# Strassen's scheme for part of the blocks of an MLP down projection, with the row scale on the activations

## The chip, the cores and the metric

The kernel runs on one core of a Trainium2 chip. The metric is device time in microseconds (us) of one execution, the median of several runs. Engines are named as in the profile: PE is TensorE's matmul stream and PEld its weight loads, DVE is VectorE, ACT is ScalarE, POOL is GpSimd, SP is SyncE, whose queue issues the loads of weights.

## The reference

Two layers over 256 tokens of width 2048: a convolution module, an MLP, latent attention, an MLP, and a last norm. Everything is float32. What the change touches is the MLP:

```python
def rms_norm(x, g):
    y = x * lax.rsqrt(jnp.mean(x * x, axis=-1, keepdims=True) + NORM_EPS)
    return y * g

def sq_relu_mlp(h, w1, w2):                      # w1: 2048 x 8192, w2: 8192 x 2048
    return jnp.square(jax.nn.relu(h @ w1)) @ w2

for layer in range(2):
    ...                                          # the token mixer
    h = rms_norm(x, norm_mlp_g[layer])
    x = x + sq_relu_mlp(h, mlp_w1[layer], mlp_w2[layer])
return rms_norm(x, final_norm_g)
```

The scale of the norm is a factor r per token, and squared ReLU lets it pass as r * r: it can be applied after the down projection, or to the squared activations.

## The kernel before

**Numbers in two parts.** Matmuls take operands in a reduced float32 form (F32R). Each operand is split in an upper part `hi` and a rest `lo = x - hi`, and a product of two operands is three matmuls (hi hi, lo hi, hi lo), added up in PSUM: `mm3`, lines 196 to 198. The split of weights is one copy on ACT (line 163) and one subtraction on DVE (line 167) for each half of a loaded piece. Pieces are 1 MB: four k-tiles of 128 rows by 512 columns. There are three buffers for raw pieces and `WB = 6` each for the upper and lower halves of a piece, so a half can be split when the half six places before it has been used.

**The MLP, `mlp` (line 453).** It works in two halves of 4096 hidden columns. In each half the up projection makes 8 groups of four blocks (128 hidden columns each); a group takes four loaded pieces and 64 pairs of matmuls (lines 476 and 477) into four banks of PSUM, with the weights as the stationary operand, so that the result is turned: hidden columns on the partitions, 256 tokens along the row. Then, for two blocks at a time, ACT and DVE add the two terms into `v` (488, 489), DVE squares after the ReLU (490), and the result is split into `gh` and `gl` (492, 493), which stay in SBUF for all groups of the half.

The down projection is `product_A` (line 398). For each of the four column blocks `n` of 512 it opens two accumulators, one per 128 tokens (`t`), and runs over the half's 32 k-tiles, in units of one loaded piece: 4 k-tiles x 2 token tiles x 3 matmuls = 24 matmuls of 128x128 by 128x512. Here the activations are the stationary operand. After a column block, `add` (line 373) adds the accumulator into the residual `xs`, multiplied by the row scale `r2`, which is worked out at the end of the first half's up projection (line 497). In the second half `prepare` also takes each finished column block on: its squares for the next norm on ACT (line 394) and, in layer 0, the block turned for the next layer (`turn_block`: 16 DVE transposes of 32x256 at line 317, then an upper part on ACT and a lower part on DVE for each of four k-tiles, lines 202 and 209). These are put into a list, `steps`, and `step(n)` sends off the next few between the units. In layer 1 the last column block is ordered by tokens and cut in halves, so that `finish` can begin early.

**Order.** The convolution and the attention have an order written out by hand. In the MLP the framework's scheduler sets each engine's order: among the instructions that it expects to be ready it takes the one that stands first in the program. Each engine then works in that order. PSUM has eight banks: six for accumulators and two for transposes from the convolution's end on (`repool`, line 964).

Of the kernel before, what the change touches and what calls it, by code (L numbers as in the profile page):

```python
# [10 lines left out]
F32 = mybir.dt.float32  # L11
F32R = mybir.dt.float32r
# [6 lines left out]
P = 128  # L19
# [21 lines left out]
PAD_O = 56  # L41
WB = 6
LOOK = WB // 2 - 1


SIDE = {KC - 3: 2, KC - 2: 4}
# [29 lines left out]
def trunk_kernel(  # L76
# [35 lines left out]
    def repool(name, **banks):  # L112

        psum_cx[0].close()
        psum_cx[0] = ExitStack()
        for kind, n in banks.items():
            psum[kind] = psum_cx[0].enter_context(tc.tile_pool(name=kind + name, bufs=n, space=PSUM, reuse_waits="tile"))

# [22 lines left out]
        return psum["acc"].tile([P, NB], F32, tag="acc", name=nm("acc"))  # L141

    def tr_tile():
        return psum["tr"].tile([P, NB], F32, tag="tr", name=nm("tr"))

    def load(srcs, nj, parts=1):
# [248 lines left out]

        return ssq, add, prepare

    def product_A(w, k_lo, nk, hi, lo, add, prepare, blocks=range(NNB), due=(), finish=None, before=None):


        due = list(due)
        for n in blocks:
            ps = [acc_tile() for _ in range(T)]

            n_end = 3 if finish is not None and n == blocks[-1] else 0
            wjs = []

            def products(u, t, to_end=True):
                for j in range(4):
                    k = 4 * u + j  # L410
                    mm3(ps[t], hi(k, t), lo(k, t), *wjs[u](j), k == 0, k == nk - 1 - 4 * (not to_end))

            for u in range(nk // 4):
                wjs.append(load_split([rows(w, k_lo + 4 * u, 4, n * NB, NB)], 4))
                if u < nk // 4 - n_end:
                    for j in range(4):
                        k = 4 * u + j
                        for t in range(T):
                            mm3(ps[t], hi(k, t), lo(k, t), *wjs[u](j), k == 0, k == nk - 1)
                while due:  # L420
                    prepare(due.pop(0))
                step(-(-20 * 4 // nk) + 1 if nk > 4 * NNB else 6)
                if u == 0 and n_end:
                    before()
            if n_end:
                for t in range(T):


                    halves = t == T - 1
                    for u in range(nk // 4 - n_end, nk // 4 - halves):  # L430
                        products(u, t, not halves)
                    add(n, ps, t)
                    if not halves:
                        prepare(n, t)
                    else:
                        h = NB // 2
                        for c in range(2):
                            o = acc_tile()[:, :h]
                            for j in range(4):
                                k = nk - 4 + j  # L440
                                wh, wl = (w[:, c * h : (c + 1) * h] for w in wjs[-1](j))
                                mm3(o, hi(k, t), lo(k, t), wh, wl, j == 0, j == 3)
                            add(n, {t: o}, t, c)
                            prepare(n, t, c)
                    finish(t)
            else:
                for t in range(T):
                    add(n, ps, t)
                due.append(n)
        while due:  # L450
            prepare(due.pop(0))

    def mlp(layer, ssq, next_gain, finish=None, before=None, beside=None):

        with ExitStack() as cx:
            mp = cx.enter_context(tc.tile_pool(name=f"mp{layer}", bufs=1, reuse_waits="tile"))
            nkh = FF // P // HALVES
            r2 = small.tile([P, T], F32, tag="r2", name=nm("r2"))
            nssq = None
            turned = None if next_gain is None else mp.tile([P, NB // P, S], F32, name=nm("turned"))  # L460
            for hf in range(HALVES):
                hh, hl = [], []
                for g in range(nkh // 4):
                    ps = [acc_tile() for _ in range(4)]
                    c0 = (hf * nkh + 4 * g) * P
                    for u in range(KC // 4):
                        if u == KC // 4 - 1:
                            step()
                        wj = load_split([rows(mlp_w1[layer], 4 * u, 4, c0, NB)], 4)
                        for j in range(4):  # L470
                            k = 4 * u + j
                            wh, wl = wj(j)
                            for b in range(4):
                                bs = slice(b * P, (b + 1) * P)

                                nc.tensor.matmul(ps[b], wh[:, bs], xhl(k), start=k == 0, stop=False)  # L476
# [5 lines left out]
                    gh = mp.tile([P, 4, S], F32R, tag="gh", name=nm("gh"), bufs=nkh // 4)  # L482
                    gl = mp.tile([P, 4, S], F32R, tag="gl", name=nm("gl"), bufs=nkh // 4)
                    for b2 in range(2):
                        v = mp.tile([P, 2, S], F32, tag="v", name=nm("v"), bufs=2)
                        for b in range(2):
                            o = ps[2 * b2 + b]
                            nc.scalar.activation(v[:, b, :], o[:, S:], AF.Copy)  # L488
                            nc.vector.tensor_tensor(v[:, b, :], o[:, :S], v[:, b, :], op=ALU.add)
                        nc.vector.scalar_tensor_tensor(out=v, in0=v, scalar=0.0, in1=v, op0=ALU.max, op1=ALU.mult)  # L490
                        bs = slice(2 * b2, 2 * b2 + 2)
                        nc.scalar.activation(gh[:, bs, :], v, AF.Copy)
                        nc.vector.tensor_tensor(gl[:, bs, :], v, gh[:, bs, :].bitcast(F32), op=ALU.subtract)
                    hh.append(gh)
                    hl.append(gl)
                if hf == 0:
                    r = rms_rstd(ssq[:, :, :NNB], NNB, D, "n")
                    nc.vector.tensor_tensor(r2, r, r, op=ALU.mult)
                nssq, add, prepare = residual_stage(
                    hf == HALVES - 1, next_gain, r2, turned, () if turned is None else range(NNB - 1)  # L500
                )
                product_A(
                    mlp_w2[layer],
                    hf * nkh,
                    nkh,
                    lambda k, t: hh[k // 4][:, k % 4, t * P : (t + 1) * P],
                    lambda k, t: hl[k // 4][:, k % 4, t * P : (t + 1) * P],
                    add,
                    prepare,
                    finish=(lambda t: finish(nssq, t)) if finish is not None and hf == HALVES - 1 else None,  # L510
                    before=lambda: before(nssq),
                )
            return nssq


# [1151 lines left out]
```

## Time and profile before

| | |
|---|---|
| time, median of 3 runs (lowest to highest) | 1975.28 us (1975.23 to 1975.32) |
| span of the profiled execution, first to last instruction (it has no time of its own beside it) | 1973.7 us |
| mean granted TensorE clock | 0.999 |
| DMA traffic | 367.58 MB, mean 186 GB/s |
| layer 0's MLP in the span (up, down, up, down) | from 300.3 to 1003.5 us |
| layer 1's MLP in the span | from 1262.3 to 1965.9 us |

The span is divided by engine into busy shares; a busy PE counts overlapping matmuls once. "x" is a count, and in a group's row the numbers are busy time and the mean duration in ns of one instruction, then the idle time of the engine just before the group's instructions and what ended it. In the rows of windows, each engine has its busy time and number of instructions, followed by the granted clock, the share of DMA time and GB/s. A row of a timeline has start, length, engine, line, operation, and what was written from what.

### The profile page before, as it was taken

The page shows a single profiled execution, that of the slowest core. Times are in us where ns is not written, and L with a number is a line of the kernel's source. Part 1 is how long each engine was busy: PE and PEld are TensorE (multiplying, and loading weights), DVE is VectorE, ACT ScalarE, POOL GpSimd, SP SyncE. Part 2 cuts the span into 40 slices and gives each one's busy share as a digit, 9 for nine tenths or more (in the row PEclk, how much of TensorE's full clock was granted, in tenths as well). Part 3 has the DMA queues.
Part 4 walks back from the last instruction along what each step waited for, and adds up shares of the span by engine and source line. Part 5 has one row for each costly group of instructions (what it writes and reads, how often), then busy time and mean ns, then how long its engine had stood idle before and what let it go on. Part 6 is the DMA issues. An engine that isn't in the chain of part 4 may idle for free.

```text
span 1973.7 us, 27791 instructions
## 1 busy us (share of the span) xinstructions
PE 1958.3 (99%) x10963; PEld 1716.5 (87%) x10963; DVE 1267.0 (64%) x1920; ACT 987.3 (50%) x1426; POOL 220.7 (11%) x172
## 2 busy tenths in 40 slices
PE   8999999999999999999999999999999999999998
PEld 8999888888888888888899998888888888888887
DVE  7999987755444556666656666866555445665554
ACT  5667755544333445444456655554443334544442
POOL 6999100000000000000002310000000000000000
PEclk9999999999999999999999999999999999999999
DMA  7765556565556666556554445666555566665553
GB/s 231 208 189 175 181 181 205 187 189 191 194 196 194 188 189 188 192 190 197 187 182 140 138 150 173 209 195 192 192 192 192 192 192 192 192 192 192 192 192 107
DMA packets 243875, 367.58 MB, mean 186 GB/s; under 512 B 15512, under 2 KB 90528, under 8 KB 243488
## 3 DMA queue, kind: packets, MB, share of 16 engines
q1 hardware_dynamic: 242416, 363.28, 57.7%
q10 hardware_dynamic: 1328, 2.52, 0.4%
q8 instruction: 86, 1.41, 0.3%
q14 instruction: 45, 0.37, 0.0%
HBM read 363.68 MB, written 2.10 MB: 185 GB/s over the span
## 4 chain that ended last, share of the span: by engine, by line
PE 95%; DVE 2%; ACT 1%; DMA 0%; issue 0%; POOL 0%; ACTq 0%; DVEq 0%
PE acc L476 23%; PE acc L196 15%; PE acc L198 15%; PE acc L197 15%; PE acc L477 12%; PE acc L581 8%; PE acc L1044 2%; DVE sum L668 1%; DMA xs<-in_x 0%; PE acc L1427 0%; PE tr L260 0%; ACT hi L163 0%; PE acc L1291 0%; PE acc L1293 0%; PE acc L1292 0%
## 5 line engine op out<-in xcount | busy, mean ns | idle before, releaser
L167 DVE TENSOR_TENSOR lo<-raw,hi 128x1024 fp32r<-128x1024 f32 (+1 forms) x631 | 760.8, 1211 | 637.4 <-ACT hi L163 632.3
L163 ACT ACTIVATE hi<-raw 128x1024 fp32r<-128x1024 f32 (+1 forms) x696 | 722.2, 1045 | 759.5 <-PE acc L197 428.1
L476 PE MATMUL acc<-xt,hi 128*128 128x512 f32 x2048 | 710.2, 390 | 0.0
L477 PE MATMUL acc<-xt,lo 128*128 128x256 f32 x2048 | 577.5, 282 | 0.0
L476 PEld LDWEIGHTS acc<-xt,hi 128*128 128x128 f32 x2048 | 384.4, 188 | 80.6
L197 PE MATMUL acc<-hi,gl 128*128 128x512 f32 (+1 forms) x1028 | 399.1, 388 | 0.0
L198 PE MATMUL acc<-lo,gh 128*128 128x512 f32 (+1 forms) x1028 | 399.1, 388 | 0.0
L196 PE MATMUL acc<-hi,gh 128*128 128x512 f32 (+1 forms) x1028 | 399.1, 388 | 0.0
L477 PEld LDWEIGHTS acc<-xt,lo 128*128 128x128 f32 x2048 | 387.1, 189 | 0.2
L198 PEld LDWEIGHTS acc<-lo,gh 128*128 128x128 f32 x1028 | 193.0, 188 | 40.1
L196 PEld LDWEIGHTS acc<-hi,gh 128*128 128x128 f32 x1028 | 193.0, 188 | 39.8
L197 PEld LDWEIGHTS acc<-hi,gl 128*128 128x128 f32 x1028 | 193.0, 188 | 39.3
L581 PE MATMUL acc<-xt,hi 128*128 128x256 f32 x1024 | 180.1, 281 | 0.3 <-ACT b L863 0.2
L668 DVE SCALAR_TENSOR_TENSOR sum<-ub,w_dw,sum 128x256 f32<-128x256 f32 x409 | 164.3, 483 | 3.5 <-ACT sum L638 3.0
L167 POOL TENSOR_TENSOR lo<-raw,hi 128x1024 fp32r<-128x1024 f32 x65 | 155.0, 2410 | 17.5 <-ACT hi L163 17.5
L581 PEld LDWEIGHTS acc<-xt,hi 128*128 128x128 f32 x1024 | 154.6, 188 | 1.1 <-ACT xt L847 0.6
L581 PE MATMUL acc<-xt,lo 128*128 128x256 f32 x512 | 139.2, 279 | 0.0
L581 PEld LDWEIGHTS acc<-xt,lo 128*128 128x128 f32 x512 | 94.6, 188 | 0.0
L1222 POOL MEMSET pad_kv<- 128x8 f32 x1 | 0.1, 106 | 770.5 <-DVE xt L209 770.5
L488 ACT ACTIVATE v<-acc 128x256 f32<-128x256 f32 x128 | 46.3, 381 | 25.4 <-PE acc L477 25.4
L196 PE MATMUL acc<-hi,oh 128*128 128x512 f32 x128 | 50.6, 395 | 0.0
L198 PE MATMUL acc<-lo,oh 128*128 128x512 f32 x128 | 50.0, 390 | 0.0
(279 smaller groups left out, 1719.9 us busy)
## 6 DMA issues: line engine op xcount, KB each, us to landing
raw<-in_mlp_w SPq DMA_DIRECT2D x256, 1024.0 KB, 5.1
raw<-in_conv_w_pw SPq DMA_DIRECT2D x62, 512.0 KB, 5.0
raw<-in_conv_w_pw SPq DMA_DIRECT2D x16, 1024.0 KB, 5.0
raw<-in_mla_w_o SPq DMA_DIRECT2D x16, 1024.0 KB, 5.5
raw<-in_mla_w_kv_up SPq DMA_DIRECT2D x8, 1024.0 KB, 5.7
raw<-in_mla_w_in SPq DMA_DIRECT2D x8, 576.0 KB, 3.7
raw<-in_mla_w_in SPq DMA_DIRECT2D x4, 1024.0 KB
raw<-in_mla_w_q_up SPq DMA_DIRECT2D x16, 256.0 KB, 3.2
```

The lines of the kernel that those rows point to most:

```text
L163: nc.scalar.activation(hi, raw[:, js, :], AF.Copy)
L167: eng.tensor_tensor(lo, raw, hi.bitcast(F32), op=ALU.subtract)
L196: nc.tensor.matmul(ps, sh, mh, start=start, stop=False)
L197: nc.tensor.matmul(ps, sl, mh, start=False, stop=False)
L198: nc.tensor.matmul(ps, sh, ml, start=False, stop=stop)
L476: nc.tensor.matmul(ps[b], wh[:, bs], xhl(k), start=k == 0, stop=False)
L477: nc.tensor.matmul(ps[b][:, :S], wl[:, bs], xh(k), start=False, stop=k == KC - 1)
L488: nc.scalar.activation(v[:, b, :], o[:, S:], AF.Copy)
L581: nc.tensor.matmul(pss[c][b][:, :S], w[i][:, bs], (xh, xl)[j](k), start=k == i + j == 0, stop=end and k == k0 + nk - 1 and (i, j) == terms ...
L668: nc.vector.scalar_tensor_tensor(out=out, in0=ubs[c][:, w : w + S], scalar=tap(c, w), in1=base, op0=ALU.mult, op1=ALU.add)
L1044: nc.tensor.matmul(ps2[b][t], x_kt(k, t), w[:, bs], start=k == g == i == 0, stop=k == KC - 1 and i == len(group) - 1,)
L1222: nc.gpsimd.memset(pad_kv, 0.0)
```

## The change

Strassen's scheme (in Winograd's variant) multiplies a 2 x 2 by a 2 x 2 matrix of blocks with 7 block products in place of 8. Here the left matrix is two token tiles by two k-tiles of activations, and the right one is two k-tiles by two column blocks of 512 of the weights.

- `MIXED` names, for each layer and half, the groups (of four k-tiles) that are multiplied in this way: three of eight, and two of eight in layer 0's second half. A group has two quads (two k-tiles each). The other groups are plain.
- In the up projection, the squared activations are multiplied by the row scale (`r2_row`, spread over the partitions by two transposes on PE and a copy), ahead of their split. The scale is worked out after the first group instead of at the end of the half, and `add` no longer has it. For mixed groups `mixed_inputs` makes seven combinations of 128x128 per quad, four of them by sums on DVE, and splits them.
- The down projection takes column blocks in pairs, in units of two k-tiles by 1024 columns (again 1 MB). `Sums` opens eight accumulators, four for the outputs (`e`) and four that are shared between outputs (`u`). Mixed and plain units alternate while there are mixed ones. A mixed unit makes the seven combinations of weights (`mixed_weights`: four copies on ACT, four subtractions and three combinations on DVE) and 21 matmuls. `join` adds the four shared sums into the outputs, after the last mixed unit and before the last plain ones: one copy on ACT, eight additions on DVE.
- In each layer's second half, column blocks 2 and 3 go through `product_A` as before, one after the other, with the mixed units for both in between the units of column block 2.
- PSUM in the MLP is one pool of eight accumulator banks, and transposes take theirs from it; a new pool of six and two is opened for the attention.

The diff, cut to its core:

```diff
+MIXED = {(0, 0): (0, 2, 4), (0, 1): (0, 2), (1, 0): (0, 2, 4), (1, 1): (0, 2, 4)}
+N_MIXED = 3
...
     def tr_tile():
+        if "tr" not in psum:
+            return acc_tile()
...
+    def turns_on(due, prepare, n=4):
+
+        if due and not steps:
+            prepare(due.pop(0))
+        step(n)
+
+    def mixed_weights(raw):
...
+        def halves(src):
+            hi = wpool.tile(list(src.shape), F32R, tag="hi", name=nm("hi"), bufs=WB)
+            lo = wpool.tile(list(src.shape), F32R, tag="lo", name=nm("lo"), bufs=WB)
+            nc.scalar.activation(hi, src, AF.Copy)
+            nc.vector.tensor_tensor(lo, src, hi.bitcast(F32), op=ALU.subtract)
+            return [(hi[:, i, :], lo[:, i, :]) for i in range(src.shape[1])]
+
+        b11, b21 = halves(raw[:, :, :NB])
+        (b22,) = halves(raw[:, 1:2, NB:])
+        top = raw[:, 0, :].rearrange("p (c n) -> p c n", c=2)
+        low = raw[:, 1, :].rearrange("p (c n) -> p c n", c=2)
+        nc.vector.tensor_tensor(top, raw[:, :, NB:], top, op=ALU.subtract)
+        nc.vector.tensor_tensor(low[:, 1, :], low[:, 1, :], top[:, 0, :], op=ALU.subtract)
+        nc.vector.tensor_tensor(low[:, 0, :], low[:, 0, :], low[:, 1, :], op=ALU.subtract)
+        t1, t3 = halves(top)
+        t4, t2 = halves(low)
+        return b11, b21, b22, t1, t2, t3, t4
+
+    def mixed_inputs(v, fh, fl):
...
+        halves(a[:, 0:1, :], 0, 1)
+        halves(a[:, 2:4, :], 1, 2)
+        nc.vector.tensor_tensor(a22, a21, a22, op=ALU.add)
+        nc.vector.tensor_tensor(a21, a11, a21, op=ALU.subtract)
+        nc.vector.tensor_tensor(a11, a22, a11, op=ALU.subtract)
+        nc.vector.tensor_tensor(a12, a12, a11, op=ALU.subtract)
+        halves(a, 3, 4)
+
+    class Sums:
...
+            self.u = [acc_tile() for _ in range(4)]
+            self.e = [[acc_tile() for _ in range(2)] for _ in range(T)]
...
+        def mixed(self, w, k, fh, fl, end):
+
+            b11, b21, b22, t1, t2, t3, t4 = mixed_weights(load([rows(w, k, 2, self.n * NB, 2 * NB)], 2))
+            u1, u6, u7, u5 = self.u
+            work = [
+                (u1, 0, b11), (u5, 6, t1), (u7, 4, t3), (u6, 3, t2),
+                (self.e[0][0], 1, b21), (self.e[0][1], 5, b22), (self.e[1][0], 2, t4),
+            ]
+            if self.begun:
+                work = [work[i] for i in (0, 4, 5, 1, 2, 6, 3)]
+            for ps, i, (wh, wl) in work:
+                mm3(ps, fh[:, i, :], fl[:, i, :], wh, wl, self.first(ps), end and any(ps is u for u in self.u))
+
+        def plain(self, w, k, hi, lo, k0, end):
+
+            at_j = split(load([rows(w, k, 2, self.n * NB, 2 * NB)], 2), nc.vector)
+            order = [(j, c, t) for j in range(2) for c in range(2) for t in range(T)]
+            if end:
+                order.sort(key=lambda r: r[1:])
...
+        def join(self, pool):
...
+            nc.scalar.activation(a, u1, AF.Copy)
+            tt(x(0, 0), u1, x(0, 0), op=ALU.add)
+            tt(a, u6, a, op=ALU.add)
+            tt(b, u7, a, op=ALU.add)
+            tt(a, u5, a, op=ALU.add)
+            tt(x(1, 0), b, x(1, 0), op=ALU.add)
+            tt(b, u5, b, op=ALU.add)
+            tt(x(0, 1), a, x(0, 1), op=ALU.add)
+            tt(x(1, 1), b, x(1, 1), op=ALU.add)
...
+            repool(f"mlp{layer}", acc=8)
...
+                    if hf == g == 0:
+                        scales()
...
+                        nc.vector.tensor_tensor(v, v, row, op=ALU.mult)
+                        if g in mixed:
+                            mixed_inputs(v, gh[:, b2], gl[:, b2])
+                            continue
...
+                for n in range(0, NNB - 2 * last, 2):
+                    sums = Sums(n)
+                    ks = [4 * g + 2 * b for g in plain for b in range(2)]
+                    for i, k in enumerate(ks):
+                        if i < len(ms):
+                            mixed_quad(sums, i)
+                            turns_on(due, prepare)
+                        if i == len(ks) - 2:
+                            sums.join(mp)
+                        sums.plain(w, k_lo + k, hi, lo, k, i == len(ks) - 1)
+                        turns_on(due, prepare)
+                    for c in range(2):
+                        for t in range(T):
+                            add(n + c, [sums.e[i][c] for i in range(T)], t)
+                        if last:
+                            due.append(n + c)
...
+                    def between(n, u, due):
+                        if n == n2 and u < len(plain) - 1:
+                            lo_i, hi_i = (len(ms) * i // (len(plain) - 1) for i in (u, u + 1))
+                            for i in range(lo_i, hi_i):
+                                mixed_quad(sums, i)
+                                turns_on(due, prepare)
+                        if n == n2 and u == len(plain) - 1:
+                            sums.join(mp)
...
     ssq = mlp(0, ssq, g_mix[1], beside=rotary_tables)
+    repool("a", acc=6, tr=2)
```

More of the change, by code (lines that the diff above doesn't have):

```diff
@@ L429, in product_A @@
                     halves = t == T - 1
-                    for u in range(nk // 4 - n_end, nk // 4 - halves):
+                    for u in range(nu - n_end, nu - halves):
                         products(u, t, not halves)
@@ L493, in mlp @@
                         nc.vector.tensor_tensor(gl[:, bs, :], v, gh[:, bs, :].bitcast(F32), op=ALU.subtract)
[L494 to L498, printed above, removed]
                 nssq, add, prepare = residual_stage(
-                    hf == HALVES - 1, next_gain, r2, turned, () if turned is None else range(NNB - 1)
+                    last, next_gain, None, turned, () if turned is None else range(NNB - 1)
@@ L501, in mlp @@
                 )
[L502 to L512, printed above, removed]
+                w, k_lo = mlp_w2[layer], hf * nkh
```

109 lines of the change are left out of this document (91 added, 18 removed).

## The prediction

> **What bounds the kernel now.** I read the busy times, the slices, the chain of waits and then the waits of TensorE (PE) alone.
>
> ```profile
> span 1973.7 us, 27791 instructions
> ...
> PE 1958.3 (99%) x10963; PEld 1716.5 (87%) x10963; DVE 1267.0 (64%) x1920; ACT 987.3 (50%) x1426; POOL 220.7 (11%) x172
> ...
> PE   8999999999999999999999999999999999999998
> ...
> DVE  7999987755444556666656666866555445665554
> ...
> PEclk9999999999999999999999999999999999999999
> ...
> PE 95%; DVE 2%; ACT 1%; DMA 0%; issue 0%; POOL 0%; ACTq 0%; DVEq 0%
> ```
> ```profile
> PE acc L295 <- DMA stage<-in_norm_mixer_g: 4.2, 1, 4.2
> PE tr L1418 <- DVE pr L1412: 1.2, 2, 1.0
> ```
>
> PE is 95% of the chain at full granted clock, and its longest wait after the 4.2 us at the start sums to 1.2 us. So a matmul taken out of the middle is worth its whole time, as long as nothing else becomes late. The eight MLP stages, by window (up and down projection of each half, then the last down projection):
>
> ```profile
> core 0: us, PE busy (x) PEld busy (x) DVE busy (x) ACT busy (x) POOL busy (x), PEclk, DMA share, GB/s
> 300.30:477.80 177.50, 177.50 (x1025) 157.32 (x1024) 120.43 (x180) 91.42 (x123) 0.00 (x0) 1.00 0.60 190
> 477.80:652.00 174.20, 174.20 (x771) 144.25 (x770) 86.50 (x79) 69.59 (x69) 0.00 (x0) 1.00 0.59 193
> 652.00:829.50 177.50, 177.50 (x1026) 157.34 (x1025) 105.91 (x124) 85.44 (x109) 0.00 (x0) 1.00 0.60 190
> 829.50:1003.00 173.50, 173.50 (x767) 143.72 (x767) 108.15 (x137) 76.00 (x92) 0.25 (x2) 1.00 0.56 184
> ...
> 1791.00:1966.00 175.00, 174.83 (x784) 145.11 (x782) 88.71 (x97) 71.23 (x83) 0.00 (x0) 1.00 0.52 172
> ```
>
> PE fills every one of them. VectorE (DVE) has the room: 86.5 us of 174.2 in a down projection, 108.2 in the second half of layer 0, where it also turns the next layer's input. The question is therefore whether what DVE takes over still fits.
>
> **Removed: matmuls.** The down projection of one half has 32 k-tiles x 4 column blocks x 2 token tiles x 3 terms = 768 matmuls. First and last of them in layer 0's second half:
>
> ```profile
> 829.44 0.39 PE L196 MATMUL acc<-hi,gh 128*128 128x512 f32 x1
> ...
> 1003.30 0.40 PE L198 MATMUL acc<-lo,gh 128*128 128x512 f32 x1
> ```
>
> 767 steps in 173.86 us: 0.2267 us each. (The 0.39 is latency; matmuls overlap.) A product is three matmuls, 0.680 us. MIXED holds 3 + 2 + 3 + 3 = 11 groups of four k-tiles, each two quads, each quad taken for two pairs of column blocks: 44 mixed units, one product saved in each. 44 x 3 x 0.2267 = 29.9 us off PE. The Trainium skill (TensorE: Matmul & The Clock Gate, "Wait — 56ns, not 53.3ns?") gives 215.7 ns from start to start for 512 columns at full clock; this trace has 226.7 at a granted clock of 1.00. By its figure the saving would be 28.5 us; the measured pace decides.
>
> **Added on PE.** Four transposes that spread the row scale. The rows of the transposes there are bound them:
>
> ```profile
> L260 PE MATMUL tr<-ident,xs 128*128 128x128 f32 x40 | 5.8, 275 | 0.0
> ```
>
> At most 4 x 0.275 = 1.1 us, at least nothing where they overlap; I take 0.5. They wait for the small DVE chain of the norm, whose sums are ready long before the first group ends (22 us a group: 177.5 / 8), so I give that wait nothing; if the sums came only at the group's end the chain would cost PE some 2 us once a layer.
>
> **Added on DVE in the down projection.** Prices:
>
> ```profile
> L167 DVE TENSOR_TENSOR lo<-raw,hi 128x1024 fp32r<-128x1024 f32 x607 | 742.5, 1228 | 619.0 <-ACT hi L163 614.0 <-PE tr L260 2.6
> ...
> L163 ACT ACTIVATE hi<-raw 128x1024 fp32r<-128x1024 f32 x672 | 706.4, 1058 | 742.9 <-PE acc L197 411.6 <-PE acc L476 292.5 <-ACT gh L492 27.1
> ...
> L489 DVE TENSOR_TENSOR v<-acc,v 128x256 f32<-128x256 f32 x128 | 49.1, 423 | 0.0
> ...
> L493 DVE TENSOR_TENSOR gl<-v,gh 128x512 fp32r<-128x512 f32 x64 | 43.8, 685 | 0.0
> L492 ACT ACTIVATE gh<-v 128x512 fp32r<-128x512 f32 x64 | 40.5, 633 | 6.4 <-DVE v L490 6.4
> ...
> L371 DVE TENSOR_TENSOR xs<-acc,xs 128x512 f32<-128x512 f32 x16 | 10.8, 690 | 2.1 <-PE acc L198 1.7 <-PE acc L1044 0.4
> ```
>
> A plain unit (1 MB of weights, 24 matmuls) costs PE 5.44 us and DVE two subtractions, 2.46 us. A mixed unit costs PE 21 matmuls, 4.76 us, and DVE four operations of 1024 columns (three subtractions, one combination) and three of 512: 4 x 1.228 + 3 x 0.685 = 6.97 us. ScalarE (ACT) goes from 2.1 to 3 x 1.058 + 0.633 = 3.8 us. A mixed and a plain unit together: DVE 9.43 us, PE 10.20. Back to back, DVE starts come closer than the durations:
>
> ```profile
> 325.50 0.42 DVE L489 TENSOR_TENSOR v<-acc,v 128x256 f32<-128x256 f32 x1
> 325.96 0.69 DVE L490 SCALAR_TENSOR_TENSOR v<-v 128x512 f32<-128x512 f32 x1
> 326.57 1.22 DVE L167 TENSOR_TENSOR lo<-raw,hi 128x1024 fp32r<-128x1024 f32 x1
> 327.70 0.68 DVE L493 TENSOR_TENSOR gl<-v,gh 128x512 fp32r<-128x512 f32 x1
> ```
>
> 0.61 for a 512, 1.13 for a 1024: the pair then takes 8.6 us. A join adds eight DVE operations out of PSUM, 8 x 0.69 = 5.5 us, per pair of column blocks. For a half with three mixed groups: 86.5 + 12 x (6.97 - 2.46) + 11.0 = 151.6 us of DVE in 174.1 - 8.2 = 165.9 us: 91% by durations, some 84% back to back. For layer 0's second half with two: 108.2 + 8 x 4.51 + 11.0 = 155.3 in 168.6, 92%. So it fits on average, and stalls can only come from places.
>
> Place one, entry to the down projection, four times. DVE works off the last group's activations first:
>
> ```profile
> 477.41 1.12 DVE L489 TENSOR_TENSOR v<-acc,v 128x256 f32<-128x256 f32 x3
> ...
> 483.00 0.68 DVE L493 TENSOR_TENSOR gl<-v,gh 128x512 fp32r<-128x512 f32 x1
> ```
>
> 6.3 us with two weight subtractions inside, plus two row multiplications, 1.4: 7.7. Then the second mixed unit: its combined weights come 5.3 to 5.7 us later, at 13.0 to 13.4; PE wants them 4.76 + 5.44 + 3 x 0.68 = 12.2 us after the entry. 0 to 1.2 us; I take 0.7, so 2.8 in all.
>
> Place two, column block 2 in layer 0's second half, where turned blocks come in between:
>
> ```profile
> L317 DVE STREAM_TRANSPOSE turned<-xs 32x256 f32<-32x256 f32 x48 | 20.9, 436 | 0.7
> ...
> L209 DVE SCALAR_TENSOR_TENSOR xt<-turned,vecs,xt 128x256 fp32r<-128x256 f32 x12 | 5.3, 480 | 0.0
> ```
>
> Six plain and four mixed units (42.6 us), two turned blocks (2 x (16 x 0.436 + 4 x 0.480) = 17.8) and four additions (2.8) make 63 us of DVE, 58 back to back, beside 6 x 5.44 + 4 x 4.76 = 51.7 us of PE. The excess of 6 to 11 meets the lead that six weight buffers allow: two units, 10.9 us, less the last copy and subtraction, 2.3: 8.6. 0 to 2.9 us; I take 1.5.
>
> **Added in the up projection, hidden.** A row multiplication per two blocks, 16 x 0.685 = 11.0 us a half, and for mixed groups four sums of 128 columns and a subtraction in three pieces instead of one. The one row of that size:
>
> ```profile
> L923 DVE TENSOR_TENSOR ca<-sum,half x2: 281/286/292, 206.5 to 206.7; 128x128 f32<-128x128 f32 x2
> ```
>
> 4 x 0.286 + 0.286 + 0.423 = 1.85 us, six times: 11.1. DVE goes from 120 to 143 us of 177.5 at worst, still under PE; I cost it at nothing, and with that cover gone it is 22 us a half.
>
> **Buffers and queues.** Weights keep their bytes; in the alternation a megabyte is asked for every 5.10 us instead of 5.44, and the DMA share of 0.59 becomes 0.63. A mixed unit holds its raw buffer to its last subtraction, and SP's next load waits behind that.
>
> ```profile
> raw<-in_mlp_w SPq DMA_DIRECT2D x256, 1024.0 KB, 5.1
> ```
>
> By the order of the six weight buffers a mixed unit is split about 9.4 us after the unit two ahead of it started; the load queued behind it serves the unit three later, more than 10 us off, and takes 5.1. Nothing, or up to 5.1 us a unit if DVE lags that far, which is the first rival. The new PSUM pools (eight banks in the MLP) could hold the first matmuls until the last two additions are done, 2 x 0.69 = 1.4 us at each of three changes; half the banks or more are long free, so I take nothing. The scale leaves the final additions: under 0.1 us on the tail.
>
> **Sum.** 1973.7 - 29.9 + 0.5 + 2.8 + 1.5 = 1948.6 us of span. The profiled execution shows only its span; the runs' median is 1975.28, 1.6 above it. So 1950.2; I say 1950.
>
> **Rivals.**
>
> *DVE becomes the bound (slower).* The place is the alternation of mixed and plain units, the mechanism the order inside a mixed unit: combine, copy on ACT, subtract. Today DVE stands waiting for ACT's copy again and again:
>
> ```profile
> DVE lo L167 <- ACT hi L163: 632.3, 442, 2.3
> ```
>
> That is 1.43 us a time, harmless now. If three of a mixed unit's four copies (1.06 us each) lay open on DVE, the pair would take 9.43 + 3.2 = 12.6 us, and a pair of column blocks 6 x 12.6 + 4 x 2.46 + 12 x 0.69 = 93.7 us; PE needs 83.0 there after the change and 16 x 5.44 = 87.0 before. 6.7 us over before, 7.3 such pairs (44 / 6): 2024 us. It decides from 2.1 us of open waiting per mixed unit. For it: 9.43 against 10.20 by durations is thin. Against it: two 512-column combinations lie over the one copy and a 1024-column subtraction over the other, and buffers free early. 0.17.
>
> *Part of the same (less gain).* One copy in each mixed unit open, 1.06 us: pair 10.5 against 10.2, within the lead in most stretches, and another 12 us lost around the joins and turned blocks. About 1962. 0.13.
>
> *The seam (no change).* A set of sums takes all eight banks; the next set's first four products need the banks that the join empties. If DVE reached the join only at the seam, PE would wait 8 x 0.69 + 0.63 for the copy, 6.2 us, at each of eight sets at worst, 49 us; at four of them, 25 us, and the time is 1975. It decides from 3.1 us a seam. Against it: the join's operands are ready four plain units, 21.8 us, before the seam in most sets, and DVE has 12 us free there (21.8 less four plain units' 9.8). The Trainium skill (Perfetto Trace Analysis, "Matmuls") wants independent matmul groups to rotate through banks so that emptying one overlaps the next; here none is left to rotate to. No wait in this trace shows what that costs. 0.06.
>
> **How the numbers follow.** Forecast 0.64 (own range 1945 to 1957: no stall at all gives 1973.7 - 29.9 + 1.6 = 1945.4; the upper bounds of the two places, the transposes and the pools, 4.8 + 2.9 + 1.1 + 4.2, give 1958 if all meet, so 1957), less gain 0.13, no change 0.06, slower 0.17. A measurement tells 0.2%, 4 us, from no change. Faster 0.77, same 0.06, slower 0.17. The range runs from 1944 over the less gain and half of no change to 1976; it leaves out the slower case.
>
> **What would show it.** Right: 132 fewer matmuls of 512 columns; down projections of about 167, 171, 167 and 168 us with PE busy throughout; DVE at 84 to 92% in them; no PE wait on a weight subtraction beyond 2 us at an entry. Wrong: PE waits on DVE in every mixed unit (DVE bound), or on the join's last operations at the start of each set (the seam), or a lower clock in the down projections.

## The result, and the profile after

| | before | after |
|---|---|---|
| time, median of 4 runs (lowest to highest), us | 1975.30 (1975.23 to 1976.29) | 1955.19 (1954.93 to 1955.42) |
| after over before, 95% interval | | 0.9896 (0.9882 to 0.9910) |
| span of the profiled execution, us | 1973.7 | 1953.6 |
| PE instructions | 10963 | 10835 |

The kernel became 1.0% faster: 20.1 us, by the times and by the spans. The forecast was 1950. From the page of after, the busy times, the slices of DVE, and the chain of waits by engine:

```profile
span 1953.6 us, 28331 instructions
...
PE 1932.2 (99%) x10835; PEld 1691.2 (87%) x10835; DVE 1547.1 (79%) x2400; ACT 1058.6 (54%) x1568; POOL 220.5 (11%) x172
...
DVE  7999988877988676787966665876788876778896
...
PE 47%; ACT 1%; DVE 1%; POOL 0%; issue 0%; DVEq 0%; ACTq 0%
```

128 PE instructions fewer are 132 matmuls out and four transposes in. DVE went from 1267 to 1547 us, 79% of the span, and PE is still the engine that is always busy. The chain of before covered the span; here its shares add up to 49%: followed back from the end, it was lost in the attention, and it says nothing of layer 0. So the waits of PE have to be read for themselves (engine and line, what it waited for, us in total, times, longest):

```profile
PE acc L203 <- DVE lo L490: 2.6, 2, 1.6
...
PE acc L201 <- DVE xt L214: 1.2, 1, 1.2
PE acc L203 <- DVE lo L172: 0.9, 1, 0.9
```

Left out are the two rows of before, which are still there. The new ones are three waits on a subtraction of weights (`lo`, lines 490 and 172) and one on a turned block (`xt`). The windows tell the stage (up and down projection of layer 0's first half, the down projection of its second half, then the two down projections of layer 1; window edges are rounded to about half a microsecond):

```profile
core 0: us, PE busy (x) PEld busy (x) DVE busy (x) ACT busy (x) POOL busy (x), PEclk, DMA share, GB/s
300.30:478.00 177.70, 177.70 (x1027) 157.53 (x1026) 138.59 (x233) 93.38 (x136) 0.00 (x0) 1.00 0.59 184
478.00:644.50 166.50, 166.50 (x738) 137.86 (x737) 143.11 (x153) 88.08 (x95) 0.00 (x0) 1.00 0.64 210
...
822.00:996.50 174.50, 170.66 (x742) 138.15 (x740) 148.71 (x192) 87.02 (x110) 0.18 (x2) 1.00 0.57 187
1435.50:1602.00 166.50, 166.50 (x737) 137.91 (x736) 143.08 (x153) 87.98 (x95) 0.00 (x0) 1.00 0.64 210
1779.00:1946.00 167.00, 166.10 (x745) 137.83 (x743) 144.72 (x171) 88.04 (x108) 0.00 (x0) 1.00 0.56 186
```

Three of the four down projections are PE from end to end, 166.5 to 167 us where they had 174 to 175. The one in layer 0's second half isn't: PE is busy for 170.66 of 174.50, and that stage became no shorter than it was in 173.5 us of before, in spite of 24 matmuls fewer. Its first and last matmul, and the two longest waits, from the timeline of PE:

```profile
821.29 0.39 PE L201 MATMUL acc<-hi,sh 128*128 128x512 f32 x1
...
939.17 0.39 PE L202 MATMUL acc<-hi,sl 128*128 128x512 f32 x1
940.54 0.50 PE L203 MATMUL acc<-lo,sh 128*128 128x512 f32 x1 [0.97 <-DVE lo L490]
...
953.44 0.50 PE L203 MATMUL acc<-lo,sh 128*128 128x512 f32 x1 [1.60 <-DVE lo L490]
...
996.29 0.39 PE L203 MATMUL acc<-lo,sh 128*128 128x512 f32 x1
```

From 821.29 to 996.29 are 175.0 us; 743 steps (744 matmuls) of 0.2267 would be 168.4. So 6.6 us are lost there, nearly all of it (6.4) between 939 and 976. Such a sum is worth more than the column of waits: that shows 2.6 + 0.9 = 3.5 us in the waits of 0.9 us and over, but a wait also costs the overlap of the matmuls around it (939.17 to 940.54 is 1.37, 1.14 over the pace, with 0.97 shown), and more than a dozen short stops of 0.1 to 0.25 us are in no row.

DVE in the same stretch, windows (DVE's busy time and instructions, granted clock, DMA share, GB/s) and timeline:

```profile
902.40:961.00 58.60, 57.24 (x84) 1.00 0.46 152
961.00:991.00 30.00, 29.02 (x43) 1.00 0.56 175
```
```profile
902.40 1.40 DVE L376 TENSOR_TENSOR xs<-acc,xs 128x512 f32<-128x512 f32 x2
...
908.92 1.83 DVE L490 TENSOR_TENSOR lo<-raw,hi 128x1024 fp32r<-128x1024 f32 x2
...
934.00 1.83 DVE L490 TENSOR_TENSOR lo<-raw,hi 128x1024 fp32r<-128x1024 f32 x2
...
937.47 0.69 DVE L498 TENSOR_TENSOR raw<-raw 128x512 f32<-128x512 f32 x1
938.19 0.43 DVE L322 STREAM_TRANSPOSE turned<-xs 32x256 f32<-32x256 f32 x1
...
946.91 1.83 DVE L490 TENSOR_TENSOR lo<-raw,hi 128x1024 fp32r<-128x1024 f32 x2
...
959.48 0.68 DVE L568 TENSOR_TENSOR xs<-acc,xs 128x512 f32<-128x512 f32 x1
...
966.55 0.68 DVE L575 TENSOR_TENSOR xs<-v,xs 128x512 f32<-128x512 f32 x1
```

For 88 us DVE never stops. It begins column block 2 with the additions and eight transposes of the block before, 6.5 us, ahead of the first mixed unit's subtractions. Then one mixed unit, one plain unit and eight turned steps take it 946.91 - 934.00 = 12.9 us, beside the 10.2 us of PE. The small lead is used up at 939. From 959.48 to 967.23 come the eight additions of the join, with other work between them; right behind them PE waits 0.9 us for a subtraction of weights (line 172).

At the end of that stage, the change to the attention (PE and DVE, timeline):

```profile
996.79 0.44 PE L265 MATMUL acc<-ident,xs 128*128 128x128 f32 x2
...
999.30 1.66 DVE L214 SCALAR_TENSOR_TENSOR xt<-acc,vecs,xt 128x256 fp32r<-128x256 f32 x4
...
1000.33 0.38 PE L201 MATMUL acc<-hi,xt 128*128 128x288 f32 x1 [1.18 <-DVE xt L214]
```

PE transposes the last block, has a few matmuls of the attention, and stands until DVE has read the transposed block out of the accumulator bank (`xt<-acc`). PE's starts are 3.05 us behind the pace at this change; before it was 0.6.

The books: 132 x 0.2267 = 29.9 us gained; 0.5 for the transposes (as predicted, not measured by itself), 6.6 in layer 0's second half and 3.05 - 0.6 = 2.45 at the change to the attention given back. That leaves 20.4; 20.1 were measured.

### The profile page after: what moved, and what is told of

Same layout as the page of the kernel before. It is cut to its first block, busy times and chain, and to the rows that moved or that the text cites. A ratio compares the mean times of both kernels' runs of the same rounds, so it can differ in the third digit from the quotient of the medians.

```text
span 1953.6 us, 28331 instructions
## 1 busy us (share of the span) xinstructions
PE 1932.2 (99%) x10835; PEld 1691.2 (87%) x10835; DVE 1547.1 (79%) x2400; ACT 1058.6 (54%) x1568; POOL 220.5 (11%) x172
## 5 line engine op out<-in xcount | busy, mean ns | idle before, releaser
L172 DVE TENSOR_TENSOR lo<-raw,hi 128x1024 fp32r<-128x1024 f32 (+2 forms) x543 | 647.9, 1205 | 294.7 <-ACT hi L168 290.8
L168 ACT ACTIVATE hi<-raw 128x1024 fp32r<-128x1024 f32 (+2 forms) x608 | 622.8, 1040 | 462.6 <-PE acc L615 238.7
L489 ACT ACTIVATE hi<-raw 128x1024 fp32r<-128x1024 f32 (+1 forms) x176 | 164.0, 949 | 179.8 <-DVE raw L497 70.1
L203 PE MATMUL acc<-lo,gh 128*128 128x512 f32 (+1 forms) x644 | 250.2, 388 | 1.1 <-DVE lo L172 0.9
L201 PE MATMUL acc<-hi,gh 128*128 128x512 f32 (+1 forms) x644 | 249.7, 388 | 0.0
L202 PE MATMUL acc<-hi,gl 128*128 128x512 f32 (+1 forms) x644 | 249.7, 388 | 0.0
L490 DVE TENSOR_TENSOR lo<-raw,hi 128x1024 fp32r<-128x1024 f32 (+1 forms) x176 | 188.5, 1087 | 34.2 <-ACT hi L489 30.6
L203 PE MATMUL acc<-lo,sh 128*128 128x512 f32 x404 | 157.8, 391 | 2.8 <-DVE lo L490 2.6
L201 PE MATMUL acc<-hi,sh 128*128 128x512 f32 x404 | 157.4, 390 | 0.0
L202 PE MATMUL acc<-hi,sl 128*128 128x512 f32 x340 | 132.4, 389 | 0.0
```

The costliest lines, as they stand in the source:

```text
L168: nc.scalar.activation(hi, raw[:, js, :], AF.Copy)
L172: eng.tensor_tensor(lo, raw, hi.bitcast(F32), op=ALU.subtract)
L201: nc.tensor.matmul(ps, sh, mh, start=start, stop=False)
L202: nc.tensor.matmul(ps, sl, mh, start=False, stop=False)
L203: nc.tensor.matmul(ps, sh, ml, start=False, stop=stop)
L489: nc.scalar.activation(hi, src, AF.Copy)
```

## The experiments

The main theory (A): the 6.6 us are place two of the prediction, DVE's work in column block 2 of layer 0's second half, and nothing else in the new scheme costs much. Against it: the pairs, banks, row scale and pools cost by themselves (B); the waits come with each mixed unit there, from the turned steps that stand inside its chain of combinations, some 1.6 us a unit (C); the turned work is too much in total, wherever it stands. For the change to the attention: the new pool (D), or the order in which the last block comes (E). Every kernel was timed in three rounds beside the kernel before, whose median was 1975.27 to 1975.43. "PE's lag" below is the sum of its starts behind the pace, worked out as above.

**No mixed groups at all.** All units are plain; column blocks in pairs, eight banks, row scale and pools as in the changed kernel.

```diff
-MIXED = {(0, 0): (0, 2, 4), (0, 1): (0, 2), (1, 0): (0, 2, 4), (1, 1): (0, 2, 4)}
+MIXED = {(0, 0): (), (0, 1): (), (1, 0): (), (1, 1): ()}
...
-                        if i == len(ks) - 2:
+                        if ms and i == len(ks) - 2:
```

> No group is mixed; pairs of column blocks, eight banks and the row scale on the activations stay. Theory A (the 9.4 us that the saving of 29.9 lost are 6.3 us of PE waiting in the second pair of column blocks of layer 0's second half, where DVE has more work than PE, some 2.5 us where the MLP's pool gives way to the attention's, and half a microsecond of transposes): 1975.3 + 0.5 + 2.5 = 1978.3 us, with no PE wait inside the MLP. Rival B (pairs, eight banks or the row scale cost PE time all along the MLP): 1981 us or more, with PE waits in several of the MLP's stages.

Measured: 1976.38 us (1976.27 to 1977.37), ratio 1.0006 (0.9997 to 1.0016). PE's lag in layer 0's MLP is 0.14 us, at the attention 1.24. So all that surrounds the seven products costs about 1 us, and B falls. Theory A's own 1978.3 was too high by 1.9: it had put the whole 2.5 us at the attention down to the new pool, of which 0.64 (1.24 less the 0.6 of before) came. The turned blocks alone don't make the waits. From here the changed kernel follows: 1976.4 - 29.9 + 6.3 + 1.8 = 1954.6, with 1955.2 measured.

**No mixed groups in layer 0's second half.** 24 matmuls more than in the changed kernel, 5.4 us.

```diff
-MIXED = {(0, 0): (0, 2, 4), (0, 1): (0, 2), (1, 0): (0, 2, 4), (1, 1): (0, 2, 4)}
+MIXED = {(0, 0): (0, 2, 4), (0, 1): (), (1, 0): (0, 2, 4), (1, 1): (0, 2, 4)}
...
-                        if i == len(ks) - 2:
+                        if ms and i == len(ks) - 2:
```

> No group is mixed in layer 0's second half, the other halves as in the change. Theory A: 8 mixed units less give back 8 x 0.68 = 5.4 us of PE work, and the 6.3 us of waits go: 1955.2 + 5.4 - 6.3 = 1954.3 us. Rival B (the waits there come from the pairs and the row scale, not from mixed units): they stay, 1960.6 us.

Measured: 1952.11 us (1952.03 to 1952.33), ratio 0.9883 (0.9868 to 0.9898): 3.1 us less than with the mixed groups. Lag 0.14 in the MLP and 1.24 at the attention: +5.4 - 6.3 - 1.8 = -2.7. Theory A had expected 1954.3, without the 1.8 at the attention. In this half the seven products lose more than they give.

**Three mixed groups in layer 0's second half,** 12 matmuls fewer, 2.7 us.

```diff
-MIXED = {(0, 0): (0, 2, 4), (0, 1): (0, 2), (1, 0): (0, 2, 4), (1, 1): (0, 2, 4)}
+MIXED = {(0, 0): (0, 2, 4), (0, 1): (0, 2, 4), (1, 0): (0, 2, 4), (1, 1): (0, 2, 4)}
```

> Three mixed groups in layer 0's second half instead of two. Theory A, with DVE's total in that pair as the bound: 4 mixed units save 2.7 us of PE; in the second pair two of them bring DVE 2 x (6.4 - 2.3) = 8.2 us more and PE 1.4 us less, so waits grow by 9.6: 1955.2 - 2.7 + 9.6 = 1962 us. Rival C (not the total, but the turned steps that stand inside each mixed unit's chain, some 1.6 us a unit): six such units for four, waits grow by 3.2: 1955.7 us. If DVE did not bind there at all: 1952.5 us.

Measured: 1959.29 us (1958.77 to 1960.12), ratio 0.9919 (0.9905 to 0.9934). The waits of PE in it:

```profile
PE acc L201 <- ACT hi L489: 3.6, 5, 1.2
PE acc L203 <- DVE lo L490: 2.3, 2, 1.2
PE acc L203 <- DVE lo L172: 1.7, 1, 1.7
```

The lag in the MLP doubles, from 6.4 to 12.6 us, and takes 6.2 for the 2.7 that it gives. The waits grow with DVE's load, but the size came out between the two expectations: by the time nearer A's 1962, by the lag (6.2 us more, some 1.7 of them from a lowered clock, see the last section) nearer C's 3.2 than A's 9.6. So this run doesn't tell A from C. The five waits on ACT's copy are read as DVE's too, since the copy of a combined piece comes after DVE's combination; no run separates the two.

**Turned blocks later.** The same work in total: after a unit of column block 2, two turned steps are sent off instead of four, and seven instead of four in column block 3, where there are plain units only.

```diff
+PACE = (2, 7)
...
-                    turns_on(due, prepare)
+                    turns_on(due, prepare, pace.get(n, 4))
...
-                                turns_on(due, prepare)
+                                turns_on(due, prepare, PACE[0])
...
-                        begun=sums.begun, beside=between,
+                        begun=sums.begun, beside=between, pace={n2: PACE[0], n2 + 1: PACE[1]},
```

> Same work; in column block 2 of the second halves two turned steps instead of four after each unit, in column block 3 seven. Theory A: DVE then has about 51 us beside 51.7 us of PE in column block 2, and 37 beside 32.6 in block 3, where its lead of up to 8.6 us covers the difference: the waits go, 1949 us, up to 1951 if 2 us remain. Rival C (steps inside the chains): half the steps, half the waits, 1952 us. If only the total of both blocks counted: unchanged, 1955 us.

Measured: 1950.18 us (1949.97 to 1950.33), ratio 0.9873 (0.9857 to 0.9890). The waits of PE that remain beyond those of before:

```profile
PE acc L266 <- DVE xs L377: 1.5, 2, 1.3
...
PE acc L202 <- DVE xt L215: 1.0, 1, 1.0
```

No wait on weights is left; the lag in the MLP is 0.9 instead of 6.4, and 0.9 us more stand at the attention (3.95). The work is all there, in another place, and 5.0 us come back. This run shows A: it is the place, not the sum, and no price that goes with each mixed unit. By a price of the steps inside its chain, half of the waits would have stayed.

**One pool.** The attention goes on with the MLP's eight banks; everything else as changed.

```diff
-    repool("a", acc=6, tr=2)
```

> The attention keeps the MLP's pool of eight banks and takes its transposes from it; nothing else is changed. Theory D (the 2.5 us at the seam to the attention come from the new pool: its first accumulators lie on banks that the last additions and the last turned block still read): PE's waits there fall from 3.0 us to the 0.6 of before, 1952.7 us. Rival E (they come from DVE being late and from its order there, with the pool or without): the waits stay, 1955.2 us.

Measured: 1953.17 us (1953.07 to 1953.55), ratio 0.9888 (0.9872 to 0.9905). In its waits of PE the three on weights are the changed kernel's to the tenth, and the `xt` row is gone. The lag at the attention goes from 3.05 to 0.80, that in the MLP stays at 6.41. DVE has the same order there and is no earlier; it begins to read the transposed block 0.14 us later than in the changed kernel (999.30), and PE no longer waits for it:

```profile
999.44 1.66 DVE L214 SCALAR_TENSOR_TENSOR xt<-acc,vecs,xt 128x256 fp32r<-128x256 f32 x4
```

So a late DVE (E) isn't the cause and falls. The new pool costs 2.0 to 2.25 us, at one of the three changes of pools. PE's own order changed with the pool: six of the eight transposes now stand behind four matmuls of the attention. Neither the pool nor that order is enough alone: without mixed groups there, the same new pool, with all eight transposes first, goes with 1.24. That it depends on which bank is read last would fit, and isn't shown.

**Help from POOL.** In column blocks 2 and 3 of layer 0's second half, POOL makes the second subtraction of each plain unit.

```diff
-        parts = [split_half(raw, h, eng) for h in range(2)]
+        parts = [split_half(raw, h, (second or eng) if h else eng) for h in range(2)]
...
-                        begun=sums.begun, beside=between,
+                        begun=sums.begun, beside=between, second=None if layer else nc.gpsimd,
```

> In column blocks 2 and 3 of layer 0's second half POOL makes the second half of the plain units' subtractions (12 of 2.4 us each), DVE the rest. PE's order and the turned steps are as in the change. Theory A (DVE's total binds there): 12 x 1.13 = 13.6 us less DVE work against 6.3 us of waits, which go: 1949 us. Rival C (the steps inside the mixed units' chains): those chains are untouched, the waits stay, 1954 to 1955 us. If POOL slowed DVE down, more than 1955.

Measured: 1956.39 us (1956.18 to 1956.89), ratio 0.9904 (0.9889 to 0.9919). DVE's and POOL's subtractions there, timeline:

```profile
917.61 1.23 DVE L172 TENSOR_TENSOR lo<-raw,hi 128x1024 fp32r<-128x1024 f32 x1
917.67 3.42 POOL L172 TENSOR_TENSOR lo<-raw,hi 128x1024 fp32r<-128x1024 f32 x1 [13.98 <-ACT hi L168]
...
940.72 2.38 POOL L172 TENSOR_TENSOR lo<-raw,hi 128x1024 fp32r<-128x1024 f32 x1 [8.34 <-ACT hi L168]
...
940.93 3.25 DVE L172 TENSOR_TENSOR lo<-raw,hi 128x1024 fp32r<-128x1024 f32 x1
```

Where DVE's subtraction begins first it keeps its 1.23 us and POOL's takes 3.42 instead of 2.4; where POOL's is under way, DVE's takes 3.25 and loses 2.0 us. Seven DVE instructions with two operands in SBUF lost 1.6 to 2.2 us each in this way, 13.8 in all, against the 13.6 taken off DVE. The relief never came, so this run doesn't tell A from C. The lag in the MLP became 7.6 us, some 1.7 of it from a lowered clock (last section).

**Both repairs: turned blocks later, one pool** (e7 in the expectations below). The edits of those two runs together:

```diff
+PACE = (2, 7)
...
+                        begun=sums.begun, beside=between, pace={n2: PACE[0], n2 + 1: PACE[1]},
...
-    repool("a", acc=6, tr=2)
```

> The turned steps moved later (two and seven after a unit) together with the kept pool. Theories A and D: 1950.2 less 3.4 us of the seam, 1946.8 us. Rival E: DVE is later at the seam with the steps moved, the 3.9 us of waits there stay, 1950.2 us.

Measured: 1948.12 us (1947.86 to 1948.44), ratio 0.9862 (0.9847 to 0.9877). This beats both kernels: 7.1 us under the changed one. The two repairs add up (5.0 + 2.0), so they are two causes. What is left at the seam, from PE's timeline:

```profile
992.23 0.44 PE L266 MATMUL acc<-ident,xs 128*128 128x128 f32 x2 [1.28 <-DVE xs L377]
```

With the turned work behind it, DVE comes to the last addition 1.3 us after PE wants its result.

**Four mixed groups in layer 0's first half,** on top of both repairs. The last mixed unit then stands just ahead of a set's last plain unit, with the join between them. The larger operands need room: a buffer of the convolution (`w_dw`) is given back after it.

```diff
-MIXED = {(0, 0): (0, 2, 4), (0, 1): (0, 2), (1, 0): (0, 2, 4), (1, 1): (0, 2, 4)}
+MIXED = {(0, 0): (0, 2, 4, 6), (0, 1): (0, 2), (1, 0): (0, 2, 4), (1, 1): (0, 2, 4)}
...
-                        if i == len(ks) - 2:
+                        if i == max(len(ks) - 2, len(ms) - 1):
...
-        w_dw = const.tile([P, W * KC], F32, name="w_dw")
+        w_dw = cv.tile([P, W * KC], F32, name="w_dw")
```

> On the kernel of e7: four mixed groups of eight in layer 0's first half (the depthwise weights' buffer moves to the convolution's own pool to make room). Mixed and plain units then alternate to the end of each pair and the join stands before the last plain unit. Theory A by totals: DVE has 8 x 6.35 + 8 x 2.27 + 7.3 = 76 us beside 8 x 10.2 = 82 us of PE in a pair, it fits; 4 mixed units more save 2.7 us: 1945.4. The seam (the next set's banks wait for the join, 4.9 us back to back and 0.6 for the copy, which can begin only 5.4 us before the seam, among DVE's other work): up to some 3 us a seam at two seams, 1945 to 1951.

Measured: 1962.4 us (1960.26 to 1963.97), ratio 0.9933 (0.9919 to 0.9948). This total says nothing of four groups, since other stages became longer. The matmuls of the up projections in both kernels (min, median and max ns, first to last start), first the two repairs alone, then with four groups:

```profile
L616 PE MATMUL acc<-xt,hi x512: 390/390/482, 300.2 to 477.6; 128*128 128x512 f32 x171
L616 PE MATMUL acc<-xt,hi x512: 390/390/399, 643.8 to 821.0; 128*128 128x512 f32 x171
```
```profile
L617 PE MATMUL acc<-xt,hi x512: 392/396/481, 305.0 to 485.7; 128*128 128x512 f32 x171
L617 PE MATMUL acc<-xt,hi x512: 392/392/397, 652.6 to 829.7; 128*128 128x512 f32 x171
```

The convolution ends 4.8 us later, and the first half's up projection takes 180.7 us instead of 177.4, with the same matmuls; so does the first up projection of layer 1 (1259.8 to 1440.5, against 1250.7 to 1428.1). Between the two up projections, which is the down projection in question, lie 652.6 - 485.7 = 166.9 us against 643.8 - 477.6 = 166.2: 2.7 us of matmuls fewer, and nothing gained. One wait took it, on ACT, and DVE stands behind that:

```profile
569.31 1.28 DVE L377 TENSOR_TENSOR xs<-acc,xs 128x512 f32<-128x512 f32 x2
570.51 0.68 DVE L500 TENSOR_TENSOR raw<-raw 128x512 f32<-128x512 f32 x1
```
```profile
571.30 1.06 ACT L490 ACTIVATE hi<-raw 128x1024 fp32r<-128x1024 f32 x1 [6.73 <-DVE raw L500]
```

The join and the four final additions hold DVE, and the weight combination of the next set's mixed unit comes after them; PE waits 2.9 us. This is the seam of the prediction's third rival, at 3.05 us of lag, in a kernel that has the join next to it. Four groups with all addresses left as they were have not been tried.

**Another pace:** three steps and six, on top of both repairs.

```diff
-PACE = (2, 7)
+PACE = (3, 6)
```

> As e7, with three turned steps after a unit in column block 2 and six in block 3 (two and seven in e7). Theory A: DVE has about 56 us beside 51.7 in column block 2, within its lead of 8.6, and 33 beside 32.6 in block 3, so that it is not behind at the last additions: the 0.8 us left in the blocks and most of the 1.4 us before the last transposes go, 1946 to 1947 us. If the lead is smaller than I take it, waits of 1 to 3 us come back in column block 2: 1948 to 1950.

Measured: 1950.95 us (1950.10 to 1952.24), ratio 0.9876 (0.9859 to 0.9892). With one step more after each unit than in the best version, PE waits once, near the border of column blocks 2 and 3:

```profile
PE acc L204 <- DVE lo L173: 2.8, 1, 2.8
```

The lag in the MLP is 5.7 us, of which the wait is half; most of the rest is a lower clock behind it (below). The time lies above both values expected. It says that the lead with which DVE enters that stretch is less than the 8.6 us that the prediction gave it, and that three steps a unit are already too many.

## Why the prediction came out as it did

- **Removed matmuls: right.** 132 matmuls at 0.2267 us, 29.9 us. The three undisturbed down projections run at that pace to the end.
- **Row scale, transposes, the new work in the up projection: right.** DVE is at 138.6 of 177.7 us there, within the "120 to 143" of the prediction, and the stage didn't grow by more than 0.2 us. Without mixed groups all the surroundings cost 1.1 us.
- **Place one, the entry, 2.8 us: too high, it cost nothing.** DVE's timeline at the first entry (PE begins the down projection at 477.85):

```profile
481.20 1.21 DVE L490 TENSOR_TENSOR lo<-raw,hi 128x1024 fp32r<-128x1024 f32 x1
482.34 0.68 DVE L643 TENSOR_TENSOR gl<-v,gh 128x512 fp32r<-128x512 f32 x1
...
490.18 1.23 DVE L490 TENSOR_TENSOR lo<-raw,hi 128x1024 fp32r<-128x1024 f32 x1 [1.21 <-ACT hi L489]
```

 The step took the mixed unit's work to begin after the last activations; the scheduler put it in between (481.20 ahead of 482.34). The last subtraction still ends 13.6 us after the entry, near the 13.0 to 13.4 of the prediction, yet no product waited: PE ran that unit from 488.06 to 492.82. The step had the last combinations wanted fourth of the seven, 12.2 us after the entry. By the order in the kernel (the line after `if self.begun` in the diff) the fourth and fifth product take `t1` and `t3`, the first pair to be combined; `t4` and `t2` come sixth and seventh, from 4.76 + 5.44 + 5 x 0.68 = 13.6 us on, just when they are ready.
- **Place two, 1.5 us (0 to 2.9): the mechanism was right and the size was wrong; 6.6 us.** The stage was put at about 171 us and took 175.0. Three sizes made the difference. DVE's work was put at 63 us, or 58 by starts that lie closer than durations; but between a transpose and a 512-column combination the starts lie 0.72 apart (937.47 to 938.19), not 0.61, and it never stopped from 902 to 990. From 902.40 to 959.48 it does all that the step lists but the first two plain units, which were ready before: 57.1 us, and 61.6 with them, 9.9 over PE's 51.7 and near the upper end of the 6 to 11. The lead was put at 8.6 us by counting weight buffers, but DVE spends its first 6.5 us there on the block before, while PE comes to the two units that are ready. PE begins column block 3 at 962.03, 4.7 us behind the pace, which leaves 5.2 for it (an estimate, 9.9 - 4.7). And the step left out the join, eight additions that DVE makes from 959.48 to 967.23, though the total of the half has them: the other 1.9 us are lost in column block 3, the one long wait there right behind the join. No run takes the join out by itself. The runs with no and with three mixed groups there give 0.14 and 12.6, and the later turned blocks 0.9.
- **New pools, 0 us (up to 1.4 at each of three): 2.0 to 2.25 at one of them,** the change to the attention, and no wait of PE in the rows at the others. The cover named ("half the banks or more are long free") didn't hold there; which bank PE waited for wasn't followed.
- **The rivals.** DVE as the bound did not come: DVE at 85 to 87% in the down projections and no wait there outside place two. The seam did not come in the changed kernel, for the reason given against it: the join's last addition in the first set stands at 543.3 and the set ends at 560.9, three plain units later. The run with four groups shows that it comes when that distance is gone. Less gain (1962) was the neighbour of what happened, but by another way: not one copy in each mixed unit, but one stretch of 40 us.
- **The sum with the measured terms:** 1973.7 - 29.9 + 0.5 + 0 + 6.6 + 2.45 = 1953.4, for a span of 1953.6. Three terms were off by -2.8, +5.1 and +2.45, which together make the 5 us between the forecast and the result. That it isn't nearly 8 is luck: the 2.8 us that the entry didn't take hid part of what place two and the pool cost.

## What to carry to other kernels

Taking matmuls off a PE that is always busy gives their whole time, but the work that pays for it has to fit stretch by stretch: here 85% of DVE over a stage hid a stretch of 40 us in which it was short, and moving other work out of that stretch gave another quarter of the gain (5.0 us beside 20.1) without any work removed. List all the work that falls into the stretch; here the join was left out. A lead isn't the number of buffers: look at what the helping engine does first when the stretch begins. And where banks must be emptied before the next set begins, keep that work several units ahead of the seam.

## What the runs showed of the hardware

**A short wait can cost a lower clock behind it.** In three of the profiled executions the granted clock falls to 0.50 for 3.41 us in layer 0's second half. Windows of that length (PE's busy time and matmuls, granted clock, DMA share, GB/s), first with three mixed groups, where a wait of 1.19 us ends at 954.87, then with the pace of three and six, behind its wait of 2.8 us:

```profile
951.94:955.35 3.41, 1.74 (x7) 1.00 0.04 14
955.36:958.77 3.41, 3.41 (x10) 0.50 0.26 57
```
```profile
964.97:968.38 3.41, 1.15 (x5) 1.00 0.00 0
968.39:971.79 3.40, 3.40 (x10) 0.50 0.65 199
```

In the lowered window a matmul of 512 columns takes 0.43 us from start to start instead of 0.23; the window costs about 1.7 us (an estimate: half of 3.41). With four groups a wait of 2.9 us lowers nothing; it lies across two windows:

```profile
567.40:570.82 3.42, 2.12 (x10) 1.00 0.00 0
570.82:574.23 3.41, 1.82 (x8) 1.00 0.00 0
```

So the length of the wait doesn't decide alone; where it falls does. The lowered windows begin a whole number of 3.4133 us after the record's first full clock: with three groups 9.864 + 277 x 3.4133 = 955.35, with the other pace 9.236 + 281 x 3.4133 = 968.37. In the run with POOL's help a window with seven matmuls (from 941.35) is followed by a lowered one, and one with eight (from 955.01) is not; nor is the one with eight in the changed kernel (from 951.03). So in these traces, in windows that hold matmuls of 512 columns alone, seven or fewer lowered the next window and eight or more did not. The Trainium skill (TensorE: Matmul & The Clock Gate, "What's actually happening") has a free-running window of 3413 ns; the traces agree with that. It names an idle window as the condition for the lower clock; here five to seven matmuls stood in the window before.

**DVE and POOL side by side.** The subtraction with two operands in SBUF went from 1.23 to 3.25 us where POOL's, of 2.4 us, had begun before it; where DVE began 0.06 us ahead it was POOL's that took longer, 3.42 us. The Trainium skill (SBUF — State Buffer, "Who interferes with whom") says that a DVE instruction with two SBUF inputs contends with a GpSimd instruction that reads SBUF; the trace agrees.

**Where a buffer lies.** With one small buffer of the convolution moved, the first up projection of each layer went from 177.4 to 180.7 us, at the same matmuls; in layer 0 their median was 396 for 390 ns. In layer 0 the operands of the mixed groups grew as well; in layer 1 they did not. What of the moved addresses does it is open.
